# Turn order, buffers and pools of the first layer's experts, and the clearing of the rates' weights

## Chip and metric

One core of one Trainium2 chip runs the whole program. The metric is the device time of one execution in microseconds (us); it is the median of the runs, given with the lowest and the highest.

## What is computed

A hybrid diffusion trunk of two layers (`DEPTH` = 2) over 512 latent tokens (`SEQ`) and 256 context tokens (`CTX_LEN`) of width 1024, all in float32. Each layer has two sub-layers, each behind an RMSNorm that the condition modulates:

1. three token mixers on one input projection (differential attention with axial rotary, RWKV-7 in both directions, a gated convolution of width 3), gated, merged and projected;
2. a mixture of 16 SwiGLU experts of width 1024. Every expert picks its own tokens: of n tokens the 2n/16 with the highest router softmax, so 64 latent tokens, and in the first layer 32 context tokens besides (the last layer has no use for its context).

```
aff = softmax(h @ router_w); gate, idx = top_k(aff^T, cap)
hid = silu(h[idx] @ w1) * (h[idx] @ w3)
out[idx] += (hid @ w2) * gate
```

The RWKV decays and rates of each direction come from low-rank products, `tanh(wl) @ w_up` and `al @ a_up`, both of rank 64.

## The kernel before

Activations stay in SBUF by blocks of 128 tokens, two of context and four of latents. A scheduler that simulates the time line sets the order of the instructions on each engine; `high_priority` raises a piece. Pools of buffers are opened and closed as a stack; a buffer that takes over another's memory waits for that one's last use.

A layer runs `rwkv_phase`, `attention`, `merge` (branches, output projection, routing of the latents) and `experts`.

**Rates.** `lora` makes the tile `ups` (`[128, 2, 2, 128]`): in part 0 the upper 64 partitions hold `w_up`, in part 1 the lower 64 hold `a_up`; the other halves must be zero, since one product over 128 partitions with `wal` (decay ranks above, rate ranks below) gives the decay from part 0 and the rate from part 1. It is cleared once in a layer, on GpSimd (L485). `load` (L509, L510), inside `pair`, brings the parts for each pair of heads by SP's queue, and `rates` multiplies them into a bank `bk`.

**Routing, first layer.** `merge` opens `xq` (seven buffers `xn` of normalised rows), `rt` (router scratch) and, in PSUM, `rtps` (`psrt`). `route` transposes a block (`pht`), multiplies it with the router's weights (`lg`) and writes `xn` to DRAM (`xnd`). `router` makes the softmax, transposes it (`pat`), takes the top 64 or 32 per expert, and turns the positions back (`ppt`, then `post` on VectorE). The latents' part runs in `merge`, the context's at the start of `experts`.

**Experts.** Groups of four experts: `pick` builds one-hot matrices `gl` and `gc` (L1607, L1615), `group_gates` turns them into gates and token numbers (`pga`, `at`) and transposes (`pgt`, `pgc`), then gathers three tiles of 128 rows from `xnd` by an indirect DMA of GpSimd (`xg`, six buffers). `gather` transposes them (`pxi`) into `xin`, with K on the partitions and, per expert, 64 latent and 32 context columns.

Per expert, `hidden` runs the two input matrices and `output` the third. Each matrix is read in four quarters of 256 rows, 1 MB each, by `load_e` through SP's queue into one of six buffers `we`; w1 and w3 go together. The stationary operand is the expert's tokens, the moving one 512 columns of weights. A latent matmul has 64 stationary columns: w1's result goes to PSUM partitions 0 to 63 of `ph`, w3's to 64 to 127. A context matmul has 32 columns and four places in `pc`. `output` does the same with `py` and `pyc`, after `phd` has transposed the hidden rows. `by_turns` sets the order of the two on each quarter: latents, context on the even ones, context, latents on the odd ones. Results of two experts are scattered back by products with `gl` transposed (`psc`), added to `xr` on VectorE.

The second layer's experts have no context (`full` is false): `by_turns` then has latents alone.

Of the kernel before, what the change touches and what calls it, by code (L numbers as in the profile page):

```python
# [8 lines left out]
F32 = mybir.dt.float32  # L9
# [10 lines left out]
P = 128  # L20
D = 1024
# [46 lines left out]
class Trunk:  # L68
# [410 lines left out]
    def lora(self, full):  # L479
        nc, rp = self.nc, self.rp  # L480
        self.wal = rp.tile([P, N], F32, name="wal", tag="wal", bufs=1)
        self.sgl = rp.tile([P, N], F32, name="sgl", tag="sgl", bufs=1)

        self.ups = rp.tile([P, 2, 2, P], F32, name="ups")
        nc.gpsimd.memset(self.ups, 0.0)  # L485

        def decay(a, n, ps):
            nc.scalar.activation(self.wal[0:64, a:a + n], ps[0:64], AF.Tanh)
            nc.vector.tensor_copy(self.wal[64:128, a:a + n], ps[64:128])

        def gate(a, n, ps):
            g = self.sgl[:, a:a + n]
            nc.scalar.activation(g, ps, AF.Tanh, scale=0.5)
            nc.vector.tensor_scalar(g, g, 0.5, 0.5, ALU.mult, ALU.add)

        return self.unit(C_WL, True, decay), self.unit(C_GL, full, gate)
# [828 lines left out]
    def merge(self, gp, full):  # L1325

        nc, tc, l = self.nc, self.tc, self.l
# [3 lines left out]
        with ExitStack() as st:  # L1331
# [11 lines left out]
            order = [b for b in (2, 3, 4, 5, 0, 1) if b * P >= a0]  # L1343
            with tc.tile_pool(reuse_waits="tile", name="br", bufs=2, side="right") as bp:
                for b, src in branches:
# [30 lines left out]
                    if b == 1:  # L1376
# [3 lines left out]
                            self.xs[x] = self.xp.tile([P, D], F32, name=f"xr{x}", tag=f"x{x}")  # L1380
                            nc.sync.dma_start(self.xs[x], self.x_src(l, x))
                        self.routing(full)
            self.xq = self.xst.enter_context(tc.tile_pool(reuse_waits="tile", name="xq", bufs=1, side="right"))
            self.xn = {b: self.xq.tile([P, D], F32, name=f"xn{b}", tag="xn", bufs=len(order) + 1) for b in order}
            self.rt = self.rst.enter_context(tc.tile_pool(reuse_waits="tile", name="rt", bufs=1, side="right"))
            wo = st.enter_context(tc.tile_pool(reuse_waits="tile", name="wo", bufs=1, side="right"))

# [10 lines left out]
            for half, blocks in ((0, lat), (1, lat), (1, ctx), (0, ctx))[:4 if full else 2]:  # L1398
                if blocks is not ctx or half == 0:
                    ws = {}  # L1400
# [117 lines left out]
    def experts(self, full):  # L1518
        nc, tc, i, l = self.nc, self.tc, self.i, self.l
# [4 lines left out]
        with ExitStack() as st:  # L1524
            if full:
                with tc.high_priority(self.route_hp):
                    for b in range(2):
                        self.route(b, self.rt)
                    self.router(1, self.rt)
            if full:  # L1530
                self.xwp = [st.enter_context(tc.tile_pool(reuse_waits="tile", name="exw", bufs=6))] * 6
                self.ew, self.n_we = {}, 0
            else:
                self.xwp += [st.enter_context(tc.tile_pool(reuse_waits="tile", name="exw2", bufs=self.exw2))] * self.exw2
# [13 lines left out]
            ahead = None  # L1548
# [74 lines left out]
    def group_gates(self, g, grp, full, aff):  # L1623

        nc, ep, psg = self.nc, self.ep, self.psg
        v = nc.vector
        gl, gc = g.gl, g.gc
        pt = psg.tile([P, 3, NE + 1], F32, name="pga", tag="g")
        self.mm_group(
            [(pt[:, pr], gl[:, b, 2 * pr:2 * pr + 2].bitcast(F32), aff[0][:, b])  # L1630
             for pr in range(2) for b in range(4)]
            + [(pt[:, 2], gc[:, b].bitcast(F32), aff[1][:, b]) for b in range(2 if full else 0)]
        )
        if full:
            at = ep.tile([P, 3], I32, name="at", tag="at", bufs=2)
            v.tensor_copy(at, pt[:, :, NE])
            g.rows = []
            for j in range(3):
                r = ep.tile([P, D], F32, name="xg", tag="xg", bufs=6)
                nc.gpsimd.indirect_dma_start(  # L1640
                    out=r[:], out_offset=None, in_=self.xnd[:, :],
                    in_offset=bass.IndirectOffsetOnAxis(ap=at[:, j:j + 1], axis=0),
                )
                g.rows.append(r)
        g.gcol = ep.tile([P, 3], F32, name="gcol", tag="gcol", bufs=2)
        for e in range(4):
            ge = 4 * grp + e
            hs = slice(64 * (e % 2), 64 * (e % 2) + 64)
            v.tensor_copy(g.gcol[hs, e // 2:e // 2 + 1], pt[hs, e // 2, ge:ge + 1])
            if full:  # L1650
                qs = slice(32 * e, 32 * e + 32)
                v.tensor_copy(g.gcol[qs, 2:3], pt[qs, 2, ge:ge + 1])
        for pr in range(2):
            pt = psg.tile([P, 4, P], F32, name="pgt", tag="g")
            for b in range(4):
                self.tr(pt[:, b], gl[:, b, 2 * pr:2 * pr + 2].bitcast(F32))
            nc.scalar.activation(g.gt[:, pr], pt.rearrange("p b t -> p (b t)"), AF.Copy)
        if full:
            pt = psg.tile([P, 2, P], F32, name="pgc", tag="g")
            for b in range(2):  # L1660
                self.tr(pt[:, b], gc[:, b].bitcast(F32))
            nc.scalar.activation(g.gct, pt.rearrange("p b t -> p (b t)"), AF.Copy)
# [42 lines left out]
    @staticmethod  # L1705
    def by_turns(latents, context, full, load, ahead=None):


        for c in range(4):
            ws = load(c)  # L1710
            if ahead and c:
                next(ahead, None)
            fs = (latents, context) if full else (latents,)
            for f in fs[::-1] if c % 2 else fs:
                f(c, *ws)

    def hidden(self, ge, full, g, ahead=None):

# [279 lines left out]
```

## Time and profile before

| | us |
|---|---|
| median of 3 runs (lowest, highest) | 3590.33 (3589.82, 3593.44) |
| the profiled execution's own time | 3593.62 |
| its span in the profile | 3591.8 |
| TensorE (PE) busy | 3332.6 (93%) |
| VectorE (DVE) busy | 1799.7 (50%) |
| ScalarE (ACT) busy | 1293.5 (36%) |
| GpSimd (POOL) busy | 1193.1 (33%) |

The profile is of one execution. A record is one instruction on an engine; its start is measured, the end of a matmul is modelled, and matmuls overlap, so the distance from one run's start to the next one's is the better measure. PEld is TensorE's weight load. PEclk is the granted clock, 1.00 at 2.4 GHz and 0.50 at 1.2 GHz. Idle time stands in brackets with what ended it. "issue" means that nothing in the profile was waited for.

### The profile page before, as it was taken

How to read it: one execution, taken by the hardware profiler on the slowest of the kernel's cores; microseconds unless marked ns; L12 is line 12 of the kernel's file. 1: busy time of each engine (PE TensorE's matmuls, PEld its weight loads, DVE VectorE, ACT ScalarE, POOL GpSimd, SP SyncE). 2: the span in 40 equal slices, each digit the busy share in tenths (PEclk: the TensorE clock that was granted, in tenths of full speed). 3: DMA queues.
4: the chain of work that ended last, by engine and by line, in shares of the span. 5: the costliest groups of instructions: out<-in, count | busy, mean ns of one | idle time of the engine just before them, and what ended most of it. 6: DMA issues, size and time to landing. Idle time of an engine off the chain costs nothing. (4 is left out here: it accounts for less than half of the span.)

```text
span 3591.8 us, 55796 instructions
## 1 busy us (share of the span) xinstructions
PE 3332.6 (93%) x20863; PEld 2243.1 (62%) x20863; DVE 1799.7 (50%) x4213; ACT 1293.5 (36%) x3234; POOL 1193.1 (33%) x1861
## 2 busy tenths in 40 slices
PE   6999999999998988999999899999899989799998
PEld 3777877777987882233333377777778968443342
DVE  5676867654665461122212556777754666412122
ACT  3455555543454221111111335556553542211111
POOL 3656565643320410000000166667654303000000
PEclk9999999999999988999999899999999989899999
DMA  5223131434106435778888620111113154599999
GB/s 179 88 70 118 36 118 58 130 116 146 48 33 215 132 124 223 292 287 327 332 312 335 216 65 28 38 38 40 45 49 102 33 180 156 211 409 409 409 409 355
DMA packets 298642, 620.92 MB, mean 173 GB/s; under 512 B 19322, under 2 KB 160596, under 8 KB 298372
## 3 DMA queue, kind: packets, MB, share of 16 engines
q1 hardware_dynamic: 294052, 604.25, 46.6%
q0 software_dynamic: 1728, 6.29, 0.5%
q10 hardware_dynamic: 2592, 6.82, 0.5%
q8 instruction: 165, 2.70, 0.3%
q14 instruction: 105, 0.86, 0.1%
HBM read 584.00 MB, written 33.29 MB: 172 GB/s over the span
## 5 line engine op out<-in xcount | busy, mean ns | idle before, releaser
L81 PE MATMUL ph<-we,xin 128*64 128x512 f32 x2048 | 514.3, 607 | 9.2 <-DVE hid L1748 5.3
L81 PE MATMUL pw<-hhi,w_hi 128*128 128x512 f32 (+1 forms) x1272 | 490.9, 390 | 20.5 <-ACT w_hi L132 8.7
L81 PE MATMUL pw<-hlo,w_hi 128*128 128x512 f32 (+1 forms) x1272 | 451.4, 359 | 0.0
L81 PE MATMUL pw<-hhi,w_lo 128*128 128x512 f32 (+1 forms) x1272 | 451.0, 360 | 0.2 <-POOL w_lo L134 0.2
L134 POOL TENSOR_TENSOR w_lo<-w_raw,w_hi 128x1024 fp32r<-128x1024 f32 x124 | 298.0, 2409 | 350.2 <-ACT w_hi L132 278.3
L81 PEld LDWEIGHTS ph<-we,xin 128*64 128x64 f32 x2048 | 150.3, 139 | 330.0 <-issue 316.0
L1853 POOL TENSOR_TENSOR ylo<-y,yhi 128x512 fp32r<-128x512 f32 x28 | 35.2, 1279 | 884.4 <-ACT yhi L1852 884.4
L735 DVE TENSOR_TENSOR wt<-slot,lvm 128x256 f16<-128x256 f32 x576 | 231.3, 419 | 133.9 <-PE slot L81 110.9
L81 PEld LDWEIGHTS pw<-hhi,w_hi 128*128 128x128 f32 x1272 | 243.4, 193 | 48.9 <-ACT w_hi L132 9.8
L81 PEld LDWEIGHTS pw<-hlo,w_hi 128*128 128x128 f32 x1272 | 243.3, 193 | 33.1 <-issue 13.9
L81 PEld LDWEIGHTS pw<-hhi,w_lo 128*128 128x128 f32 x1272 | 241.2, 191 | 33.6 <-issue 1.0
L132 ACT ACTIVATE w_hi<-w_raw 128x1024 fp32r<-128x1024 f32 x168 | 176.9, 1056 | 235.6 <-DMA w_raw<-in_w_in 68.7
L81 PE MATMUL py<-we,hT 128*64 128x512 f32 x1024 | 247.6, 604 | 7.7 <-DMA we<-in_exp_w 2.4
L752 ACT ACTIVATE xx<-slot 128x256 f16<-128x256 f32 x384 | 146.4, 382 | 162.0 <-PE slot L81 139.8
L1747 ACT ACTIVATE sl<-ph 64x512 f32<-64x512 f32 x64 | 37.7, 590 | 439.7 <-PE ph L81 421.6
L1863 DVE TENSOR_TENSOR xr<-xr,psc 128x512 f32<-128x512 f32 x144 | 90.7, 683 | 201.5 <-PE psc L81 201.4
L81 PEld LDWEIGHTS py<-we,hT 128*64 128x64 f32 x1024 | 70.3, 138 | 151.5 <-issue 134.1
L81 PE MATMUL pt<-w_hi,hhi 128*128 128x256 f32 x544 | 155.9, 288 | 4.9 <-ACT xk L1123 2.0
L81 PE MATMUL slot<-xt,wt 128*128 128x128 f16 x960 | 133.1, 224 | 28.7 <-DVE wt L735 27.5
L81 PE MATMUL pt<-w_lo,hhi 128*128 128x256 f32 x544 | 155.7, 287 | 3.5 <-POOL w_lo L134 3.5
L81 PE MATMUL pt<-w_hi,hlo 128*128 128x256 f32 x544 | 155.0, 285 | 0.0
L1748 DVE TENSOR_TENSOR hid<-sl,ph 64x512 f32<-64x512 f32 x64 | 44.2, 690 | 208.7 <-ACT sl L1747 208.2
(420 smaller groups left out, 7558.2 us busy)
## 6 DMA issues: line engine op xcount, KB each, us to landing
we<-in_exp_w SPq DMA_DIRECT2D x384, 1024.0 KB
w_raw<-in_w_in SPq DMA_DIRECT2D x124, 512.0 KB
ada_w<-in_ada_w SPq DMA_DIRECT2D x96, 512.0 KB
w_raw<-in_w_branch SPq DMA_DIRECT2D x24, 512.0 KB
w_raw<-in_w_out SPq DMA_DIRECT2D x20, 512.0 KB
gd<-gt SPq DMA_DIRECT2D x24, 384.0 KB
g<-gd SPq DMA_DIRECT2D x24, 384.0 KB
gd<-gt SPq DMA_DIRECT2D x24, 256.0 KB
```

Source lines behind the costliest of these rows:

```text
L81: return self.leg(self.nc.tensor.matmul(out, lhsT, rhs, start=start, stop=stop))
L132: nc.scalar.activation(hi, raw, AF.Copy)
L134: self.lo_eng.tensor_tensor(lo, raw, hi.bitcast(F32), ALU.subtract)
L735: v.tensor_tensor(wt, ps, self.lvm[:, :, l], ALU.mult)
L752: nc.scalar.activation(x, ps2, AF.Copy)
L1747: nc.scalar.activation(sl, ph[0:64, ns], AF.Silu)
L1748: v.tensor_tensor(hid[0:64, ns], sl, ph[64:128, ns], ALU.mult)
L1853: (v if by_block else self.ylo_eng[nh]).tensor_tensor(lo, yn, hi.bitcast(F32), ALU.subtract)
L1863: v.tensor_tensor(x, x, pt, ALU.add)
```

## The change

`by_turns` runs the latents on quarters 0 and 1, the context on 0 to 3, then the latents on 2 and 3; a quarter is loaded at its first use. The weights have eleven buffers. To make room, `xq` and the router's pools are closed before the weight pool is opened, `xn` has one buffer less in the first layer, and `xg` three buffers. In `lora` only the halves of `ups` that no load writes are cleared.

```diff
--- before.py
+++ after.py
@@ -482,7 +482,8 @@
         self.sgl = rp.tile([P, N], F32, name="sgl", tag="sgl", bufs=1)
 
         self.ups = rp.tile([P, 2, 2, P], F32, name="ups")
-        nc.gpsimd.memset(self.ups, 0.0)
+        nc.gpsimd.memset(self.ups[64:128, 0], 0.0)
+        nc.gpsimd.memset(self.ups[0:64, 1], 0.0)
 
         def decay(a, n, ps):
             nc.scalar.activation(self.wal[0:64, a:a + n], ps[0:64], AF.Tanh)
@@ -1380,8 +1381,9 @@
                             self.xs[x] = self.xp.tile([P, D], F32, name=f"xr{x}", tag=f"x{x}")
                             nc.sync.dma_start(self.xs[x], self.x_src(l, x))
                         self.routing(full)
-            self.xq = self.xst.enter_context(tc.tile_pool(reuse_waits="tile", name="xq", bufs=1, side="right"))
-            self.xn = {b: self.xq.tile([P, D], F32, name=f"xn{b}", tag="xn", bufs=len(order) + 1) for b in order}
+            self.xq = (self.rst if full else self.xst).enter_context(
+                tc.tile_pool(reuse_waits="tile", name="xq", bufs=1, side="right"))
+            self.xn = {b: self.xq.tile([P, D], F32, name=f"xn{b}", tag="xn", bufs=len(order) + 1 - full) for b in order}
             self.rt = self.rst.enter_context(tc.tile_pool(reuse_waits="tile", name="rt", bufs=1, side="right"))
             wo = st.enter_context(tc.tile_pool(reuse_waits="tile", name="wo", bufs=1, side="right"))
 
@@ -1527,8 +1529,8 @@
                     for b in range(2):
                         self.route(b, self.rt)
                     self.router(1, self.rt)
-            if full:
-                self.xwp = [st.enter_context(tc.tile_pool(reuse_waits="tile", name="exw", bufs=6))] * 6
+                self.rst.close()
+                self.xwp = [st.enter_context(tc.tile_pool(reuse_waits="tile", name="exw", bufs=11))] * 11
                 self.ew, self.n_we = {}, 0
             else:
                 self.xwp += [st.enter_context(tc.tile_pool(reuse_waits="tile", name="exw2", bufs=self.exw2))] * self.exw2
@@ -1636,7 +1638,7 @@
             v.tensor_copy(at, pt[:, :, NE])
             g.rows = []
             for j in range(3):
-                r = ep.tile([P, D], F32, name="xg", tag="xg", bufs=6)
+                r = ep.tile([P, D], F32, name="xg", tag="xg", bufs=3)
                 nc.gpsimd.indirect_dma_start(
                     out=r[:], out_offset=None, in_=self.xnd[:, :],
                     in_offset=bass.IndirectOffsetOnAxis(ap=at[:, j:j + 1], axis=0),
@@ -1706,13 +1708,16 @@
     def by_turns(latents, context, full, load, ahead=None):
 
 
-        for c in range(4):
-            ws = load(c)
-            if ahead and c:
-                next(ahead, None)
-            fs = (latents, context) if full else (latents,)
-            for f in fs[::-1] if c % 2 else fs:
-                f(c, *ws)
+        ws = {}
+        order = [(latents, c) for c in range(4)]
+        if full:
+            order[2:2] = [(context, c) for c in range(4)]
+        for f, c in order:
+            if c not in ws:
+                ws[c] = load(c)
+                if ahead and c:
+                    next(ahead, None)
+            f(c, *ws[c])
 
     def hidden(self, ge, full, g, ahead=None):
```

The rows of an order count matmuls; of the float32 ones here the profile has two records each. TensorE in the first layer's experts, the second half of one expert's hidden part and the output part after it, before (`ph`, `py`: latents; `pc`, `pyc`: context; `xin`, `hT`: the tokens):

```order
L81 MATMUL ph<-we,xin 64x512 x8
L81 MATMUL pc<-we,xin 32x512 x2
L81 MATMUL ph<-we,xin 64x512 x7
L81 MATMUL pc<-we,xin 32x512 x8
L81 MATMUL ph<-we,xin 64x512
L81 MATMUL pc<-we,xin 32x512 x6
L81 MATMUL ph<-we,xin 64x512 x7
L81 MATMUL py<-we,hT 64x512 x4
L81 MATMUL pyc<-we,hT 32x512 x8
L81 MATMUL py<-we,hT 64x512 x8
L81 MATMUL pyc<-we,hT 32x512 x8
L81 MATMUL py<-we,hT 64x512 x4
```

and one expert's hidden part and the output part after it, now:

```order
L81 MATMUL ph<-we,xin 64x512 x16
L81 MATMUL pc<-we,xin 32x512 x32
L81 MATMUL ph<-we,xin 64x512 x16
L1774 MATMUL phd<-ident,hid 128x96 x8
L81 MATMUL py<-we,hT 64x512 x8
L81 MATMUL pyc<-we,hT 32x512 x16
L81 MATMUL py<-we,hT 64x512 x8
```

The latents' first half and second half now stand together, with the whole context between them.

TensorE at the start of the first layer's experts, before (`lg`, `pht`: the context's router; `pga`, `pgt`: group 0's picking):

```order
L108 MATMUL pht<-ident,xr_13928 128x128 x4
L85 MATMUL pga<-aff_14582,gl 128x17
L108 MATMUL pgt<-ident,gl 128x128 x2
L85 MATMUL pga<-aff_14582,gl 128x17
L108 MATMUL pgt<-ident,gl 128x128 x2
L85 MATMUL pga<-aff_14582,gl 128x17
L85 MATMUL lg<-rws,h_15565 128x16 x2
L85 MATMUL pga<-aff_14582,gl 128x17
L85 MATMUL lg<-rws,h_15565 128x16
L85 MATMUL pga<-aff_14582,gl 128x17
L85 MATMUL lg<-rws,h_15565 128x16
L85 MATMUL pga<-aff_14582,gl 128x17 x3
```

and now:

```order
L108 MATMUL pht<-ident,xr_13929 128x128 x4
L85 MATMUL lg<-rws,h_15566 128x16 x4
L108 MATMUL pht<-ident,xr_13929 128x128 x4
L85 MATMUL lg<-rws,h_15596 128x16 x4
L85 MATMUL lg<-rws,h_15607 128x16 x4
L1500 MATMUL pat<-ident,aff_14584 16x128 x2
L1516 MATMUL ppt<-ident,pos 128x16 x2
L85 MATMUL pga<-aff_14583,gl 128x17
L108 MATMUL pgt<-ident,gl 128x128 x2
L85 MATMUL pga<-aff_14583,gl 128x17
L108 MATMUL pgt<-ident,gl 128x128 x2
L85 MATMUL pga<-aff_14583,gl 128x17
```

The picking moved behind the router's last transposes (`pat`, `ppt`).

SP's queue at the same place, before (`arow`, `rows`: gates and parameters of the next layer):

```order
L128 DMA w_raw<-in_w_out 128x4x256 x7
L1700 DMA we<-in_exp_w 128x2x1024 x6
L381 DMA arow<-ard_2_89 128x512
L305 DMA rows<-in_norm_g 8x128 x2
L305 DMA rows<-in_rwkv_conv_w 36x128
```

and now:

```order
L128 DMA w_raw<-in_w_out 128x4x256 x7
L1702 DMA we<-in_exp_w 128x2x1024 x11
L381 DMA arow<-ard_2_89 128x512
L305 DMA rows<-in_norm_g 8x128 x2
L305 DMA rows<-in_rwkv_conv_w 36x128
```

Five more weight loads stand ahead of the small ones. Elsewhere the order differs in the first load of `ups` in the first layer, which moved ahead of the eight loads of `arow`, and in the last heads of the second layer's attention; TensorE's order up to the first layer's experts and from the second layer's merge on is the same.

## Rows read from the trace of the kernel before

**Rows 1.** Head of the page.

```profile
span 3591.8 us, 55796 instructions
```

**Rows 2.** Stretches: us, engines' busy us (records), PEclk, DMA share, GB/s.

```profile
1420.00:2020.00 600.00, 595.02 (x3233) 191.36 (x3234) 143.86 (x248) 86.86 (x168) 33.98 (x29) 0.99 0.84 315
3150.00:3550.00 400.00, 382.51 (x1762) 153.42 (x1760) 81.90 (x143) 52.89 (x97) 17.64 (x14) 0.98 1.03 409
2890.00:2940.00 50.00, 38.38 (x223) 31.33 (x222) 39.98 (x96) 31.65 (x76) 2.81 (x6) 0.85 0.58 209
```

**Rows 3.** Timeline of TensorE, first experts: start us, us, engine, line, instruction, records.

```profile
1628.00 7.09 PE L81 MATMUL ph<-we,xin 128*64 128x512 f32 x32
1635.02 3.64 PE L81 MATMUL pc<-we,xin 128*32 128x512 f32 x32
1638.59 3.65 PE L81 MATMUL ph<-we,xin 128*64 128x512 f32 x16
1642.17 0.88 PE L1769 MATMUL phd<-ident,hid 96*128 96x96 f32 x8
```

**Rows 4.** Timeline of TensorE, another expert.

```profile
1445.11 1.05 PE L81 MATMUL pc<-we,xin 128*32 128x512 f32 x4
1446.09 3.65 PE L81 MATMUL ph<-we,xin 128*64 128x512 f32 x14
1449.67 1.92 PE L81 MATMUL pc<-we,xin 128*32 128x512 f32 x16
1451.52 1.07 PE L81 MATMUL ph<-we,xin 128*64 128x512 f32 x2
1452.52 1.91 PE L81 MATMUL pc<-we,xin 128*32 128x512 f32 x12
1454.36 3.65 PE L81 MATMUL ph<-we,xin 128*64 128x512 f32 x16
```

**Rows 5.** Groups by form, 1300 to 2150 us: busy us, mean ns, idle before.

```profile
L81 PE MATMUL ph<-we,xin 128*64 128x512 f32 x1024 | 258.5, 605 | 3.0 <-DVE hid L1748 2.8 <-ACT xin L1684 0.2
L81 PE MATMUL pc<-we,xin 128*32 128x512 f32 x1024 | 141.5, 600 | 0.0
L81 PE MATMUL py<-we,hT 128*64 128x512 f32 x512 | 128.4, 612 | 3.2 <-issue 1.8 <-DVE hT L1770 1.0 <-ACT sl L1747 0.4
...
L81 PE MATMUL pyc<-we,hT 128*32 128x512 f32 x512 | 64.5, 598 | 0.7 <-ACT hT L1770 0.7
```

**Rows 6.** Timeline of TensorE, start of the first experts.

```profile
1330.12 0.45 PE L85 MATMUL pga<-aff,gl 128*128 128x17 f32 x2
...
1334.46 1.44 PE L85 MATMUL pga<-aff,gl 128*128 128x17 f32 x6
...
1337.48 3.43 PE L85 MATMUL lg<-rws,h 128*128 128x16 f32 x16
```

**Rows 7.** Timeline of VectorE (DVE), the same start.

```profile
1336.87 1.43 DVE L1607 TENSOR_TENSOR gl<-iota,post 128x256 fp32r<-128x256 f32 x4 [1.98 <-PE pgt L108]
...
1349.15 0.19 DVE L1515 COPY post<-ppt 128x32 f32<-128x32 f32 x1 [0.55 <-PE ppt L1514]
...
1350.90 0.16 DVE L1636 CAST at<-pga 128x3 int32<-128x3 f32 x1 [1.03 <-PE pga L85]
```

**Rows 8.** Stretches at the same start, columns as in rows 2.

```profile
1330.00:1335.00 5.00, 5.00 (x27) 5.00 (x25) 1.22 (x3) 0.00 (x0) 0.00 (x0) 0.50 1.02 400
1345.00:1350.00 5.00, 0.64 (x4) 0.57 (x5) 4.04 (x13) 0.00 (x0) 0.00 (x0) 0.50 0.00 0
```

**Rows 9.** Timeline of TensorE, first `bk` of each layer; in brackets the idle time.

```profile
71.94 1.19 PE L81 MATMUL bk<-wal,ups 128*128 128x256 f32 x2 [4.67 <-DMA ups<-in_rwkv_w_up]
...
2075.61 0.67 PE L81 MATMUL bk<-wal,ups 128*128 128x256 f32 x2 [1.90 <-DMA ups<-in_rwkv_w_up]
```

**Rows 10.** Timeline of GpSimd (POOL), the clear of `ups` in each layer.

```profile
69.27 0.52 POOL L485 MEMSET ups<- 128x512 f32 x1
...
2072.99 0.52 POOL L485 MEMSET ups<- 128x512 f32 x1
```

## The prediction

> **What bounds the kernel now.** I went from the whole to one wave of matmuls. The profiled execution spans 3591.8 us [rows 1] and took 3593.62 us; the median of the runs shown, 3590.33 us, lies 3.3 us below. I read the stretches next. In the first layer's experts, from 1420 to 2020 us, TensorE is busy 595.02 of 600 us while the weights stream at 315 GB/s; in the second layer's experts, from 3150 to 3550 us, the same kind of transfer runs at 409 GB/s [rows 2]. So the changed stage is bound by TensorE and has spare transfer rate. A fully busy engine may still be badly filled, so the third view is the timeline of TensorE inside that stage. A latent matmul uses 64 columns of the array and a context matmul 32, so two latent or four context matmuls can run side by side; I call such a set a wave. Each matmul leaves two records.
>
> A run of 32 `ph` records takes 7.02 us from its start to the next run's, one of 16 takes 3.58 us [rows 3]. The 16 more records, four waves, cost 3.44 us: **0.86 us a wave**. What is left, 3.58 less four waves, is **0.14 us for each change of kind**. A context run of 32 records, four waves of four matmuls, takes 3.57 us: the same two prices. The next group shows what the order of before wastes: seven latent matmuls (14 records) take 3.58 us like eight, six context matmuls (12 records) take 1.84 us against 1.85 for eight (16 records), two of them (4 records) take 0.98 us, and a single latent one (2 records) 1.00 us [rows 4]. A wave that isn't full costs a whole wave.
>
> **The change, part by part.**
>
> *By turns.* Before, latents and context alternated on each quarter of a matrix and the scheduler cut the runs further; now the order on TensorE is mostly 16, 32, 16 matmuls in the hidden half and 8, 16, 8 in the output half. TensorE runs its instructions in that order, so I count runs and waves in both programs, from the first `ph` to the first transpose of the second layer. Both have 768 latent and 768 context matmuls; `ph` and `pc` have 1024 records each, `py` and `pyc` 512 [rows 5], two to a matmul. Before: 119 latent runs with 410 waves, 97 context runs with 216 waves. After: 58 runs with 389 waves, 46 runs with 199 waves. That is 626 - 588 = 38 waves and 216 - 104 = 112 runs less: 38 x 0.86 = 32.7 us and 112 x 0.14 = 15.7 us, together **-48.4 us**. As a check, before comes to 626 x 0.86 + 216 x 0.14 = 568.6 us, where the four groups are busy 258.5 + 141.5 + 128.4 + 64.5 = 592.9 us, tails and stretches at half clock included [rows 5].
>
> The Trainium skill ("TensorEngine Tiling (Array Packing)", Key Properties) says that a change of tiling mode drains the engine, and names no other cost of a mixed order there. By it the gain would be the 15.7 us of the runs alone; the half-filled waves above are what the trace adds to it.
>
> The other work on TensorE there (`psc`, `phd`, `pxi`) keeps its count and is only grouped otherwise; after it TensorE waits for evictions. Of such waits all kinds together leave 600 - 595.02 = 5.0 us idle [rows 2], so I take 0, between -5 and +5.
>
> *Eleven buffers.* Five more weight loads stand on SP's queue at the start, ahead of the rows and gate loads behind them. One load is 1.05 MB; at the 400 GB/s that such loads reach there [rows 8] it takes 2.6 us, five take 13.1 us. The transfers stand still from 1345 to 1350 us [rows 8], before the gather of token rows, so most of it fits. Bounds 0 and +13; I take 0, nearest to the empty row. With four quarters at most held at once by an expert, seven loads can be ahead instead of four. The stage must now move its 315 GB/s x 600 us = 189 MB in about 556 us (the stage's part of the gain taken off): 340 GB/s, under the 409 seen. So no new wait for weights.
>
> *Pools closed earlier.* Group 0's picking (`gl`, `pga`, `pgt`) now stands behind the context's router, not in the midst of it, since their buffers are the router's. Before, TensorE went from the first `pga` at 1330.12 us to the router's last 16 `lg` records at 1337.48 us [rows 6]; of these 7.36 us eight `lg` records at 3.43/16 = 0.21 us and four transposes at about the same (2.6 us) are the router's, so it now ends 4.8 us earlier. Behind the chain's end (`post`, 1349.15 us) the token numbers `at` followed 1.75 us later [rows 7]; now there is first one of four `gl` (1.43/4), then 24 records at the price of the six `pga` in 1.44 us (5.8 us at most), and the next group's four `gl` on VectorE (1.43 us [rows 7]): about 7.2 us. Net 7.2 - 1.75 - 4.8 = +0.7; I take **+1 us**, bounds -3 (VectorE's part hidden) and +3. Three gather buffers instead of six cost nothing: the old rows are transposed long before the next group's are gathered.
>
> *Clearing.* The first `bk` matmul of each layer waited for its loads, which waited for a whole clear on GpSimd: TensorE stood 4.67 us until 71.94 us, and 1.90 us until 2075.61 us [rows 9]. Now only the rows no load writes are cleared, so the loads go ahead, but the matmul still waits for the clears, which GpSimd does at the same place in its order: they started at 69.27 and 2072.99 us and took 0.52 us [rows 10]. Two halves end by 70.3 and 2074.0 us at the latest, 1.6 us sooner each. I take **-3 us**; bounds 0 (it comes back in the wait for the next product) and -6.6 (both waits gone).
>
> *The last heads of the second layer* are reordered by the scheduler near 2890 to 2940 us, where TensorE is busy 38.38 of 50 us [rows 2]. Same work, so 0; half of the idle 11.6 us either way, +-6.
>
> Sum: -48.4 + 0 + 0 + 1 - 3 + 0 = -50.4 us. Against the profiled execution that is 3543.2 us; against the median **3540 us**. That is 1.4%; a measurement of this kernel tells a change from none beyond about 0.2%, 7 us.
>
> **The rivals.**
>
> *Only the drains are saved.* If half-filled waves overlapped with what follows once the order differs, 15.7 us would remain, with -3 and +1: 3572.6 us. Against it: in rows 4 every partial run, before either kind, costs its full wave. 0.06.
>
> *Weights late.* A load waits on SP for a freed buffer, and the queue behind it waits too; with half the latents held back until the context's end, buffers come free in clumps. If arrivals ran at 330 GB/s, the 189 MB would take 573 us, 27 us less than 600 instead of 44: 3557 us. For it: 1.05 MB loads issued in clumps; against: the 409 GB/s of the second layer under the same loads. 0.11.
>
> The Trainium skill ("DMA: Bandwidth & Descriptors", Bandwidth) measures 341 GB/s for single 1 MB transfers and puts the limit of the memory per core at some 358 GB/s when its neighbour is busy too. By the first figure the stage would just be fed, with nothing over; the 409 GB/s row on this one core disagrees.
>
> *Slower.* If the weights and not the array set the pace of this stage already, 315 GB/s is its ceiling, fuller waves only turn into waiting, and the five loads at the start push the gather back by their full 13.1 us: 3590.3 + 13.1 - 3 + 1 = 3601 us. It decides as soon as the stage can't pass 315 GB/s. Against it: 409 GB/s, and almost no idle time of TensorE. 0.03.
>
> That the change doesn't do what it says is excluded for the order, which stands in the program; I leave 0.01 for what I haven't seen.
>
> **How the numbers follow.** The forecast has 0.79. Its own bounds (regrouping +-5, start -3 to +16, clearing -3.6 to +3, heads +-6) won't all fall together: some 12 us below and 14 above, 3528 to 3554. To hold 8 in 10 with part of the late weights I give 3527 to 3560. Faster by over 0.2%: the forecast, the drains alone and the late weights, 0.79 + 0.06 + 0.11 = 0.96; slower: 0.03; within 0.2%: the 0.01 left.
>
> **What would show it.** In the first layer's experts: `ph` runs of 32 records and `pc` runs of 64 without a cut, each at 0.86 us a wave; the stage about 48 us shorter, TensorE still over 98% busy, transfers near 340 GB/s, no wait of `ph` or `py` for `we`. At the start, `at` within 3 us of 1351, the weights' transfers done before the gather. The `bk` waits at 70 and before 2030 us near 3 us and near zero. I am wrong if matmuls wait for weights, if runs stay 16 and 32 but cost more than 0.86 us a wave, or if the gather lands over 5 us later.

## The result and the profile after

| | us |
|---|---|
| the changed kernel, median of 4 runs (lowest, highest) | 3529.64 (3527.93, 3537.01) |
| the kernel before, beside it, median of 4 | 3591.69 (3589.82, 3593.44) |
| ratio, 95% interval | 0.9835 (0.9823 to 0.9847) |
| profiled execution of the changed kernel | 3529.81, span 3528.0 |

The forecast was 3540 us with a range of 3527 to 3560. Run once more later (e11), on one chip with e10 and e12, the changed kernel took 3536.53 us (3532.22 to 3538.74, 4 runs) against 3589.46 (15 runs), a ratio of 0.9854 (0.9839 to 0.9869). Its single runs reach from 3528 to 3539 us; the forecast's ratio, 3540 / 3590.33 = 0.9860, lies inside the second interval and just above the first. Why executions of one program lie so far apart is a part of what follows.

The head of the page of the changed kernel, and its line of busy times; TensorE lost 63.0 us of busy time, while VectorE, ScalarE and GpSimd changed by 1.3 us at most:

```profile
span 3528.0 us, 55804 instructions
...
PE 3269.6 (93%) x20863; PEld 2235.1 (63%) x20863; DVE 1799.8 (51%) x4213; ACT 1293.9 (37%) x3234; POOL 1194.4 (34%) x1863
```

Stretches of the changed kernel, first layer's experts and second layer's (columns as in rows 2):

```profile
1400.00:1960.00 560.00, 554.67 (x3266) 195.10 (x3262) 143.01 (x248) 87.63 (x168) 33.88 (x29) 0.99 0.86 333
...
3086.00:3486.00 400.00, 382.27 (x1760) 153.21 (x1758) 81.70 (x142) 52.88 (x97) 17.66 (x14) 0.98 1.03 409
```

TensorE is busy 554.67 of 560 us, the weights stream at 333 GB/s, and the second layer still moves 409 GB/s, as in [rows 2]. The timeline of TensorE in one expert:

```profile
1510.65 7.07 PE L81 MATMUL pc<-we,xin 128*32 128x512 f32 x64
1517.65 7.09 PE L81 MATMUL ph<-we,xin 128*64 128x512 f32 x32
1524.67 0.88 PE L1774 MATMUL phd<-ident,hid 96*128 96x96 f32 x8
```

The eight context waves take 7.00 us from start to start and the eight latent ones after them 7.02 us; [rows 3] had 7.02 us for eight latent waves. The prices of a wave and a change of kind are those of before. The groups by form over the first layer's experts (1300 to 2080 us):

```profile
L81 PE MATMUL ph<-we,xin 128*64 128x512 f32 x1024 | 233.1, 598 | 3.0 <-DVE hid L1753 2.8 <-ACT xin L1686 0.2
L81 PE MATMUL py<-we,hT 128*64 128x512 f32 x512 | 122.0, 605 | 3.6 <-issue 2.6 <-DVE hT L1775 1.0
L81 PE MATMUL pc<-we,xin 128*32 128x512 f32 x1024 | 115.2, 595 | 0.0
L81 PE MATMUL pyc<-we,hT 128*32 128x512 f32 x512 | 65.1, 597 | 0.6 <-ACT hT L1775 0.6
```

Against [rows 5], `ph` fell from 258.5 to 233.1 us, `pc` from 141.5 to 115.2, `py` from 128.4 to 122.0, `pyc` stayed. Nothing waits for `we`. The records are as many as before; the time went because fewer waves run part empty and the kind changes less often.

To see where the 63.8 us of span went I cut both executions at the same instructions. In brackets: how much of the stretch the trace records at half clock, 0.50.

| from, to | before | after | after, second profile (e11) |
|---|---|---|---|
| start, first `bk` | 71.94 | 70.72 | 70.17 |
| first `bk`, last `po` (first layer's mixers) | 1247.56 (64.2) | 1240.02 (51.2) | 1241.35 (54.1) |
| last `po`, first `ph` (start of the experts) | 41.02 (36.6) | 43.23 (39.6) | 43.06 (39.0) |
| first `ph`, last `py` (the stage) | 666.79 (18.0) | 615.57 (11.6) | 619.13 (19.0) |
| last `py`, first `bk` of the second layer | 48.30 (27.3) | 46.01 (20.5) | 45.40 (17.1) |
| that `bk`, first `ph` of the second layer | 1025.04 (78.5) | 1020.78 (75.1) | 1021.23 (68.3) |
| that `ph`, end | 491.18 (18.5) | 491.67 (18.8) | 492.25 (29.1) |

The stage gives 51.2 of the 63.8 us. The mixers of the first layer give 7.5 us, though TensorE runs the same instructions there in the same order; the prediction had nothing for that stretch behind its first wait. The second layer up to its experts gives 4.3 us. In the stage TensorE is almost always busy, so a us at half clock loses half a us of work. Less half of its half-clock time the stage is 666.79 - 9.0 = 657.8 us before, 615.57 - 5.8 = 609.8 us after, and 619.13 - 9.5 = 609.6 us in the second profile. This **net stage time** is what the experiments below are read by. It fell by 48.0 us. Profiles of one order on TensorE agree in it to 0.2 us: 657.8, 657.7 and 657.7 us in before, e3 and e9, and 609.8, 609.8 and 609.6 us in the changed kernel, e4 and e11.

At the start, TensorE of the changed kernel, and VectorE from `post` to `at`:

```profile
1326.31 1.89 PE L85 MATMUL lg<-rws,h 128*128 128x16 f32 x8 [0.78 <-ACT h L1467]
...
1336.04 0.36 PE L1516 MATMUL ppt<-ident,pos 16*128 16x16 f32 x2 [5.47 <-DVE pos L1513]
1337.02 0.61 PE L85 MATMUL pga<-aff,gl 128*128 128x17 f32 x2 [0.62 <-DVE gl L1609]
...
1339.42 2.15 PE L85 MATMUL pga<-aff,gl 128*128 128x17 f32 x10
...
1349.41 0.87 PE L108 MATMUL pxi<-ident,xg 128*128 128x128 f32 x3 [6.15 <-DMA xg<-xnd,at]
```

```profile
1336.44 0.19 DVE L1517 COPY post<-ppt 128x32 f32<-128x32 f32 x1 [0.55 <-PE ppt L1516]
1336.55 1.42 DVE L1609 TENSOR_TENSOR gl<-iota,post 128x256 fp32r<-128x256 f32 x4
...
1343.47 0.15 DVE L1638 CAST at<-pga 128x3 int32<-128x3 f32 x1
```

`post` to `at` takes 7.03 us, with `gl`, twenty records of `pga` and transposes inside it, where [rows 7] had 1.75. From the last `po` to `post` it is 25.7 us for 29.6, since the picking is out of the router's way; the sum of both is 32.7 us for 31.4. At 1342 to 1344 us, before the gather, the transfers are down to 38 GB/s: the weights are in by then. At the first `bk` of each layer (TensorE, first layer; then VectorE and GpSimd beside it; then TensorE and GpSimd, second layer):

```profile
70.72 0.70 PE L81 MATMUL bk<-wal,ups 128*128 128x256 f32 x2 [2.46 <-POOL ups L485]
```

```profile
69.30 1.17 DVE L490 COPY wal<-pw 64x256 f32<-64x256 f32 x2 [5.25 <-ACT wal L489]
```

```profile
70.36 0.31 POOL L485 MEMSET ups<- 64x256 f32 x1
70.72 0.30 POOL L486 MEMSET ups<- 64x256 f32 x1
```

```profile
2015.55 0.67 PE L81 MATMUL bk<-wal,ups 128*128 128x256 f32 x2 [1.57 <-issue]
```

```profile
2013.37 0.31 POOL L485 MEMSET ups<- 64x256 f32 x1
2013.74 0.30 POOL L486 MEMSET ups<- 64x256 f32 x1
```

The wait fell from 4.67 to 2.46 us and from 1.90 to 1.57 us [rows 9]. In the first layer `bk` starts at 70.72 us, when the first clear is done (70.36 + 0.31 = 70.67 us); it doesn't wait for the second, which ends at 71.02. In the second layer both clears are done by 2014.04 us, 1.5 us before `bk`. There `bk` starts 0.1 us after the first of VectorE's two copies of `wal` is done (2015.44 us) and before the second is. The first copy of the first layer is done at 69.73 us, so clears that were done earlier could win up to some 0.9 us at the first place and nothing at the second.

### The profile page after: what moved, and what is told of

Read it like the earlier page. It is cut to its first block, busy times and chain, and to the rows that moved or that the text cites. A ratio compares the mean times of both kernels' runs of the same rounds, so it can differ in the third digit from the quotient of the medians.

```text
span 3528.0 us, 55804 instructions
## 1 busy us (share of the span) xinstructions
PE 3269.6 (93%) x20863; PEld 2235.1 (63%) x20863; DVE 1799.8 (51%) x4213; ACT 1293.9 (37%) x3234; POOL 1194.4 (34%) x1863
## 5 line engine op out<-in xcount | busy, mean ns | idle before, releaser
L81 PE MATMUL ph<-we,xin 128*64 128x512 f32 x2048 | 489.2, 603 | 9.4 <-DVE hid L1753 5.3
L757 ACT ACTIVATE xt<-slot 128x256 f16<-128x256 f32 x384 | 146.7, 383 | 0.0
```

What stands on the lines that cost most here:

```text
L81: return self.leg(self.nc.tensor.matmul(out, lhsT, rhs, start=start, stop=stop))
L757: nc.scalar.activation(xt, ps, AF.Copy)
```

## The experiments

Every kernel was counted like the two of the prediction: waves and runs of one kind in TensorE's order, in the first layer's experts. The model gives 0.86 us to a wave and 0.14 us to a run; the other work of the stage is 609.8 - (588 x 0.86 + 104 x 0.14) = 89.6 us, taken once from the changed kernel and then left alone. The net stage is that of one profile for each kernel.

| kernel | waves, runs | model, us | stage (half clock) | net stage | us by the median | ratio to before |
|---|---|---|---|---|---|---|
| before | 626, 216 | 658.2 | 666.79 (18.0) | 657.8 | 3591.69 | 1 |
| changed | 588, 104 | 609.8 | 615.57 (11.6) | 609.8 | 3529.64 | 0.9835 |
| e1: old turns, else changed | 588, 166 | 618.5 | 626.48 (15.2) | 618.9 | 3545.94 | 0.9876 |
| e2: before, new turns | 669, 268 | 702.5 | 704.00 (14.7) | 696.6 | 3624.24 | 1.0103 |
| e3: before, new clearing | 626, 216 | 658.2 | 667.07 (18.8) | 657.7 | 3584.85 | 0.9990 |
| e4: whole clear, else changed | 588, 104 | 609.8 | 619.44 (19.3) | 609.8 | 3538.54 | 0.9852 |
| e5: latent waves half empty | 584, 106 | 606.7 | 613.15 (12.9) | 606.7 | 3530.76 | 0.9839 |
| e6: more runs | 587, 162 | 617.1 | 622.83 (11.6) | 617.0 | 3546.65 | 0.9880 |
| e7: eight buffers, else changed | 611, 138 | 634.4 | 641.04 (14.2) | 633.9 | 3557.44 | 0.9908 |
| e9: before, new pools | 626, 216 | 658.2 | 666.72 (18.0) | 657.7 | 3589.49 | 1.0004 |
| e10: changed, waves tied | 576, 97 | 598.5 | 600.99 (5.9) | 598.0 | 3524.53 | 0.9824 |
| e11: changed, again | 588, 104 | 609.8 | 619.13 (19.0) | 609.6 | 3536.53 | 0.9854 |
| e12: before, waves tied | 630, 273 | 669.6 | 675.15 (11.6) | 669.3 | 3595.51 | 1.0017 |

The model is within 0.6 us of the net stage time in every kernel but e2. Each ratio is to the runs of before beside it; the intervals reach 0.0008 to 0.0019 to either side. The times expected for the kernels that are built on the changed one count from its first median, 3529.64 us. By theory A all six (e1, e4 to e7, e10) came out 3 to 10 us above them, in line with the second median, which is 6.9 us higher; so the net stage is the sharper reading.

**e1 and e2: turns or buffers?** Each undoes one of the two against one of the kernels. e1 is the changed kernel with the old loop:

```diff
-        ws = {}
-        order = [(latents, c) for c in range(4)]
...
+        for c in range(4):
+            ws = load(c)
...
+            for f in fs[::-1] if c % 2 else fs:
+                f(c, *ws)
```

> The changed kernel with the old order in by_turns (latents and context alternate on each quarter); eleven buffers, pools and clearing stay. Counted in TensorE's order of the first layer's experts, this program has 588 waves, as the changed kernel has, and 166 runs of one kind where that has 104. Theory A (a wave costs 0.86 us full or not, a change of kind 0.14 us): 62 runs more, 62 x 0.14 = 8.7 us above the changed kernel, so 3538 us; most of the gain would then come with the buffers, since with them the scheduler no longer cuts waves. Rival B (the order of the turns is what gains, the buffers only feed it): 48 us above the changed kernel, 3578 us. Rival C (each change of kind costs more than 0.14 us because the array drains): 0.3 us each would give 3548 us.

e2 is the kernel before with the new loop and nothing else (the same lines the other way).

> The kernel before with the new order in by_turns alone; six buffers, pools and clearing as before. Counted in TensorE's order, the first layer's experts have 669 waves and 268 runs, where the kernel before has 626 and 216. Theory A: 43 x 0.86 + 52 x 0.14 = 37.0 + 7.3 = 44 us slower than before, 3635 us, and more if weights come late besides. Rival B (the order itself gains): near 3543 us. The stretch from 72 to 1320 us has the same instructions as in the kernel before: if its half-clock stretches near 454, 576 and 593 us return at the same places, they belong to the program; if not, they come and go from execution to execution.

e1 kept most of the gain: its net stage is 9.1 us above the changed kernel's (8.7 expected), the median 0.9876 (0.9859 to 0.9894) of before. Rival B's 48 us are excluded. Its median lies 8 us over the 3538 us expected, and 9 us over the changed kernel's second median. By the median alone rival C (3548 us) would lie nearer; the net stage, 9.1 us up and not the 18.6 us of rival C, is against it, and e6 comes back to it. e2 is slower than before by 1.03% (1.0087 to 1.0119), its net stage by 38.9 us. So the order of the turns by itself costs 39 us with six buffers and gains 9 us with eleven; the buffers (with the pools and the clearing, which leave the net stage as it is, e9 and e3) gain 38.9 us with the old order and 86.8 with the new. The timeline of TensorE in e2 shows how (`pc` x4 is half a wave of context, `ph` x2 half a wave of latents):

```profile
1723.82 1.05 PE L81 MATMUL pc<-we,xin 128*32 128x512 f32 x4
1724.80 1.07 PE L81 MATMUL ph<-we,xin 128*64 128x512 f32 x2
1725.81 0.30 PE L1772 MATMUL phd<-ident,hid 96*128 96x96 f32 x1
1726.04 1.91 PE L81 MATMUL pc<-we,xin 128*32 128x512 f32 x12
```

0.98 us and 1.01 us from start to start, as in [rows 4]: half-filled waves again, only more of them. The chip didn't wait for weights; over 640 us of e2's stage TensorE is busy 638.08 us:

```profile
1400.00:2040.00 640.00, 638.08 (x3232) 196.94 (x3228) 141.86 (x244) 85.62 (x165) 33.88 (x29) 0.99 0.78 295
```

What the buffers change is the order that the scheduler writes. That it writes these cuts because, with six, weights are late by its own reckoning is my reading, and not tried; that the cuts are in the order and that no matmul waits for weights on the chip is what the runs show. e2 alone misses the model, by 5.9 us; TensorE is idle 5.23 us in its stage where before has 7.77, so 2.5 us of that is other work covering waits. The other 3.4 us stay open.

**e3 and e4: the clearing.** e3 adds the two smaller clears to the kernel before, e4 takes them out of the changed kernel:

```diff
-        nc.gpsimd.memset(self.ups, 0.0)
+        nc.gpsimd.memset(self.ups[64:128, 0], 0.0)
+        nc.gpsimd.memset(self.ups[0:64, 1], 0.0)
```

> The kernel before with the new clearing of ups alone. TensorE's order is that of before. Theory A: the first bk wait goes from 4.67 to about 2.5 us, the half-clock stretch behind it gets about 1 us cheaper, the second layer's wait loses 0.3 us: 3.5 us faster, 3588 us. Rival D (the whole 8.5 us by which the changed kernel is ahead at the end of the first layer's mixers comes from the clearing, by half-clock stretches that no longer occur): 9 us faster, 3583 us, with those stretches missing between 400 and 800 us.

> The changed kernel with the whole clear of ups as before. Theory A: the first bk wait is 4.7 us again, 3.5 us above the changed kernel, 3533 us. Rival D: 9 us above it, 3538.5 us, with half-clock stretches near 454, 576 and 593 us as in the kernel before.

e3 took 0.999 (0.998 to 1.0001) of before: 3.3 us by the medians, not told apart from none. Nor do e4's 3538.54 us (3531.86 to 3542.13) decide, since the changed kernel's own two medians are 7 us apart. Both medians lie nearer to rival D's numbers (3583 and 3538.5) than to theory A's, so the profiles have to decide. The first `bk` starts at 71.8 to 72.6 us in the five profiles with the whole clear and at 69.8 to 70.8 us in the eight with the small ones, 1.7 us apart by the means. The way from there to the last `po` shows no effect: 1240.5 to 1247.6 us with the whole clear, 1237.8 to 1249.1 us with the small ones, over the same instructions. Rival D falls: e2, with before's program, took 1242.32 us there for before's 1247.56, and e7, with the small clears, 1249.12 us.

What goes with the time is the half-clock share: 41.0 us of e3's 1237.83, 68.3 us of e7's 1249.12. Less half of it, the thirteen ways are 1213.1 to 1218.2 us, so it takes up about half of their spread. The half-clock stretches also answer e2's expectation: of those near 454, 576 and 593 us in before, e2 has the first two and e9 the first; with the small clears the first two stand in e1, e6, e7, e10 and e11 and are missing in e3, e5 and the changed kernel's first profile. They come and go, and the small clears don't remove them. Two stretches of four profiles show it, 570 to 600 us and the whole way from 72 to 1320 us (PEclk is the third number from the end). The kernel before:

```profile
570.00:600.00 30.00, 26.46 (x175) 21.63 (x174) 20.28 (x62) 14.01 (x41) 16.74 (x30) 0.89 0.28 89
72.00:1320.00 1248.00, 1187.30 (x8476) 1012.62 (x8476) 774.67 (x1856) 567.15 (x1501) 566.65 (x901) 0.97 0.31 98
```

e2, the same program up to the experts:

```profile
570.00:600.00 30.00, 26.71 (x192) 21.54 (x191) 20.36 (x64) 15.53 (x46) 17.52 (x34) 0.94 0.28 88
72.00:1320.00 1248.00, 1182.54 (x8478) 1008.16 (x8478) 779.88 (x1876) 568.90 (x1503) 569.55 (x902) 0.98 0.31 99
```

The changed kernel, first and second profile:

```profile
570.00:600.00 30.00, 27.35 (x206) 22.10 (x206) 22.24 (x65) 16.87 (x49) 17.56 (x34) 1.00 0.28 88
72.00:1320.00 1248.00, 1184.05 (x8490) 1009.64 (x8489) 783.21 (x1888) 568.18 (x1503) 569.86 (x903) 0.98 0.31 101
```

```profile
570.00:600.00 30.00, 27.86 (x198) 22.75 (x198) 20.60 (x61) 17.57 (x50) 15.21 (x30) 0.94 0.25 80
72.00:1320.00 1248.00, 1184.68 (x8488) 1010.30 (x8486) 781.49 (x1887) 568.09 (x1503) 569.06 (x903) 0.98 0.31 100
```

The clock of 570 to 600 us is 0.89 and 0.94 for one program, 1.00 and 0.94 for the other. The Trainium skill ("TensorE: Matmul & The Clock Gate", What's actually happening) says that the gate's watch runs freely and doesn't start with the kernel, so that the point of a change varies. These four profiles agree with it as far as they go: the clock differs between executions of one program. That this is the reason is not shown by any run here.

**e5 and e6: what a wave and a run cost.** e5 leaves w3's latent products out for most of the inner dimension, so that a wave has one latent matmul in place of two; e6 deals the context out in two pieces.

```diff
-                    self.mm(ph[64:128, ns], xl[:, k], w3[:, kk, ns], k == 0, k == 7)
+                    if not full or k in (0, 7):
+                        self.mm(ph[64:128, ns], xl[:, k], w3[:, kk, ns], k == 0, k == 7)
```

> The changed kernel, in whose first layer the w3 products of the latents are left out for the inner products 1 to 6 of 8 (192 of the 1536 latent and context matmuls of the first layer's experts; all weights are still loaded). Two consecutive w1 products then want the same columns. Theory A (a wave costs 0.86 us full or not): 584 waves and 106 runs where the changed kernel has 588 and 104, so 3 us faster, 3526 us, with a quarter of the latent work gone. Rival (each matmul has its own price, half a wave, 0.43 us): 192 x 0.43 = 82 us faster, 3447 us. Measured by the stage, first ph to last py, less half of its time at half clock: 609.8 us in the changed kernel, so 607 against 528 us.

```diff
-            order[2:2] = [(context, c) for c in range(4)]
+            C = [(context, c) for c in range(4)]
+            order = order[:2] + C[:2] + order[2:3] + C[2:] + order[3:]
```

> The changed kernel with the turns latents 0 and 1, context 0 and 1, latents 2, context 2 and 3, latents 3: waves 587 where the changed kernel has 588, runs 162 where it has 104. Theory A: 58 x 0.14 - 0.86 = 7.3 us slower, 3537 us; the stage, less half of its time at half clock, 617 us where the changed kernel has 609.8. Rival C (a change of kind costs 0.3 us): 16.5 us slower, 3546 us, stage 626 us. Rival (changes of kind are free, waves are all): 3529 us, stage 609 us.

e5's timeline of TensorE, and its `ph` group:

```profile
1511.76 7.07 PE L81 MATMUL pc<-we,xin 128*32 128x512 f32 x64
1518.77 7.08 PE L81 MATMUL ph<-we,xin 128*64 128x512 f32 x20
1525.78 0.88 PE L1775 MATMUL phd<-ident,hid 96*128 96x96 f32 x8
```

```profile
L81 PE MATMUL ph<-we,xin 128*64 128x512 f32 x640 | 230.3, 604 | 3.0 <-DVE hid L1754 2.8 <-ACT xin L1686 0.2
```

A run of 20 records takes 7.01 us where one of 32 took 7.02: eight waves both. The group has 640 records for 1024 and is busy 230.3 us for 233.1. The net stage is 606.7 us, as the wave model says, 79 us above what a price for each matmul gives. In e6 58 more runs and one wave less cost 7.2 us of net stage, (7.2 + 0.9) / 58 = 0.14 us a run: free changes and changes at 0.3 us both fall. Its median, 3546.65 us (3538.56 to 3551.89), is 10 us over the 3537 us expected; in its profile the first layer's mixers, which the edit doesn't touch, took 1247.52 us for the changed kernel's 1240.02.

**e7 and e9: buffers, pools and the start.** e7 has eight weight buffers in the changed kernel (`bufs=8))] * 8`), e9 the new pools in the kernel before (`xq` in `rst`, `rst` closed before `exw` opens, `xn` and `xg` smaller).

> The changed kernel with eight weight buffers for eleven. The program then has 611 waves and 138 runs where the changed kernel has 588 and 104. Theory A with the buffers acting through the scheduler's order: 23 x 0.86 + 34 x 0.14 = 24.5 us slower, 3554 us, stage less half of its half-clock time 634 us, without waits for weights. Rival (the buffers act by transfers that come late on the chip): TensorE idle before matmuls on weights, and the stage longer than 634 us. Start of the first layer's experts, last output projection to first ph: 43.2 us as in the changed kernel if the order of the picking costs the 2.2 us, some 41.7 us if the loads in front of the gather do (two more than before for five).

> The kernel before with the pools of the change alone: the router's pools and xn closed before the weights' pool opens, one xn buffer less, three xg buffers; six weight buffers, old turns, whole clear. The order in the stage is that of before (626 waves, 216 runs). Theory A: the start, last output projection to first ph, takes 43.2 us where before takes 41.0, the stage stays at 657.8 us less half of its half-clock time: 2.2 us slower, 3590 us. Rival (the five loads ahead of the gather cost the 2.2 us, not the pools): start 41.0 us, time that of before.

e7's net stage is 633.9 us, 24.1 above the changed kernel. Its groups show no wait for weights:

```profile
L81 PE MATMUL ph<-we,xin 128*64 128x512 f32 x1024 | 243.6, 600 | 3.0 <-DVE hid L1753 2.7 <-ACT xin L1686 0.2
L81 PE MATMUL pc<-we,xin 128*32 128x512 f32 x1024 | 131.0, 595 | 0.0
```

So the buffers act through the order alone. The start surprised me: 41.58 us in e7 and 41.49 in e9, not 43.2, and in both the picking stands in the midst of the context's router as before. TensorE and VectorE of e9:

```profile
1328.10 1.44 PE L85 MATMUL pga<-aff,gl 128*128 128x17 f32 x6
...
1331.12 3.43 PE L85 MATMUL lg<-rws,h 128*128 128x16 f32 x16
...
1350.16 0.90 PE L108 MATMUL pxi<-ident,xg 128*128 128x128 f32 x3 [5.36 <-DMA xg<-xnd,at]
```

```profile
1342.79 0.19 DVE L1515 COPY post<-ppt 128x32 f32<-128x32 f32 x1 [0.55 <-PE ppt L1514]
...
1344.55 0.16 DVE L1637 CAST at<-pga 128x3 int32<-128x3 f32 x1 [1.04 <-PE pga L85]
```

`pga` runs ahead of the router's last `lg`, and `post` to `at` takes 1.76 us. So not the closed pools but the buffers beyond eight put the picking behind the router. That its tiles then find room only in the router's memory is read from the pools and wasn't tried. Of the 2.2 us, 0.5 come with the pools (e9), the other 1.7 with the late picking. The pools as the whole cause fall. The totals lie near what the loads ahead of the gather were to give (41.0 and some 41.7 us), but the way behind the loads doesn't bear them out: from `at` to the first `pxi`, over the gather, it is 5.94 us with eleven loads (5.68 to 6.08 over seven profiles), 5.70 with eight (e7) and 5.62 with six (e9): some 0.3 us. The longer part lies before `at`, in the picking: 32.7 us from the last `po`, for 31.4 in before, e7 and e9.

**e10 to e12: waves tied.** The model has 576 waves as the least, 384 + 192. In the changed kernel's order about half of the cut waves break off at a transpose of the picking or the gathering. e10 ties a wave together:

```diff
+    def wave(self, full, mms):
+        first = self.mm(*mms[0])
+        for m in mms[1:]:
+            if full:
+                with self.tc.high_priority(self.wave_hp), self.tc.issue_after(first.ins):
+                    self.mm(*m)
...
-                    self.mm(ph[0:64, ns], xl[:, k], w1[:, kk, ns], k == 0, k == 7)
-                    self.mm(ph[64:128, ns], xl[:, k], w3[:, kk, ns], k == 0, k == 7)
+                    self.wave(full, [(ph[0:64, ns], xl[:, k], w1[:, kk, ns], k == 0, k == 7),
+                                     (ph[64:128, ns], xl[:, k], w3[:, kk, ns], k == 0, k == 7)])
```

and the same for `pc`, `py` and `pyc`, with `wave_hp` 2000. e11 is the changed kernel again, e12 the tie in the kernel before.

> The changed kernel, in which the matmuls of one wave in the first layer's experts (two latent, four context) are tied together: those behind the first are raised in priority and issued after it, so that no other work cuts a wave. Counted in TensorE's order, 576 waves and 97 runs where the changed kernel has 588 and 104; 576 is the least, 384 + 192. Theory A: 12 x 0.86 + 7 x 0.14 = 11.3 us faster than the changed kernel, 3518 us; the stage, first ph to last py, less half of its time at half clock, 598.5 us where the changed kernel has 609.8. Rival (the transfers or the evictions bind now): the stage stays above 604 us and TensorE waits for weights.

> The changed kernel once more, for a second profile and more rounds on the same chip as the version with whole waves. If the half-clock stretches between 72 and 1320 us come and go from execution to execution, this profile has others there than the first one, and the way from the first bk to the last output projection differs from 1240 us by several us; less half of the half-clock time it is again 1213 to 1218 us. The stage is 609.8 us less half of its half-clock time, the start 43.2 us.

> The kernel before with the tied waves alone: six buffers, old turns. Counted in TensorE's order, 630 waves and 273 runs where the kernel before has 626 and 216. Theory A: 4 x 0.86 + 57 x 0.14 = 11.4 us slower than before, 3600 us, the stage 669 us less half of its half-clock time: without buffers the scheduler can't keep waves whole, since it places a matmul only when its weights are there by its reckoning. Rival (the tie alone makes waves full): 43 us faster than before.

e10 beats both kernels: 3524.53 us (3523.09 to 3527.31, 5 runs), 0.9824 (0.9811 to 0.9838) of before, where e11, on the same chip beside it, took 3536.53 us. Its slowest run is 5 us below e11's fastest; against the changed kernel's first comparison (0.9835) the intervals overlap. The net stage fell by 11.8 us (11.3 expected). TensorE's timeline in one expert, and the stretch of the stage:

```profile
1500.93 7.09 PE L81 MATMUL ph<-we,xin 128*64 128x512 f32 x32
1507.95 7.07 PE L81 MATMUL pc<-we,xin 128*32 128x512 f32 x64
1514.95 7.09 PE L81 MATMUL ph<-we,xin 128*64 128x512 f32 x32
1521.97 0.88 PE L1783 MATMUL phd<-ident,hid 96*128 96x96 f32 x8
...
1526.80 3.64 PE L81 MATMUL pyc<-we,hT 128*32 128x512 f32 x32
```

```profile
1380.00:1950.00 570.00, 561.88 (x3366) 197.77 (x3366) 146.33 (x257) 88.55 (x171) 33.91 (x29) 1.00 0.87 337
```

In this expert the runs are 32, 64, 32 and 16, 32, 16 records without a cut, TensorE is busy 561.88 of 570 us, and 337 GB/s still don't bind. e11's way through the first layer's mixers, 1241.35 us, is only 1.3 us from the first profile's and not several, as expected; less half of its half-clock time it is 1214.3 us, inside the 1213 to 1218 us expected. e12 is slower than before, 1.0017 (1.0007 to 1.0026): with six buffers the tie alone leaves 630 waves and cuts more runs. The buffers come first.

## Why the prediction came out as it did

**The prices were right.** 0.86 us a wave and 0.14 us a change of kind, read off [rows 3, 4], give -48.4 us for the stage; the net stage fell by 48.0, and the two prices, with the other work taken from the changed kernel, then met the net stage of eleven further profiles to 0.6 us each (seven other orders and the changed one again), e2 excepted. "Only the drains are saved" (-15.7) falls by the stage itself and by e5; a change of kind costs 0.14 us in e6 and is the smaller part. The Trainium skill ("TensorEngine Tiling (Array Packing)", Key Properties) names a drain at a change of tiling mode; the trace agrees that such a change costs time. "Weights late" and "slower" fall by 333 GB/s without a wait for `we`.

**The step that failed is the heading above the sum.** "By turns" was given the whole -48.4 and "Eleven buffers" 0, because the counts were taken from the two finished programs and not from either edit alone. The runs share them out the other way: eleven buffers bring the waves from 626 to 588 and the runs from 216 to 166 (e1, -38.9 us of net stage), the turns the runs from 166 to 104 (-9.1). Taken first, the turns cost 38.9 us (e2), and the buffers then give 86.8; the gain is of both together. The sum didn't suffer, since a count of the finished program holds whichever edit made it.

**The start** cost 2.2 us for +1, inside its bounds of -3 and +3. The reckoning of `post` to `at` was good (7.03 us for 7.2), but the router ended 3.9 us earlier, not 4.8, and from `at` to the first `pxi` it took 5.94 us, for 5.19 before. That it came from the pools was wrong (e9). `at` came at 1343.47 us, not "within 3 us of 1351", since the last `po` already came 8.8 us earlier; between the two 1.3 us were lost.

**The clearing** was taken at -3, two times 1.6. The first layer gave 1.7 us by the means over thirteen profiles; in the second the wait fell by 0.33 us, not 1.6. The failed step is "1.6 us sooner each": it left out that `bk` also needs the first copy of `wal`, which ended the wait in the second layer (2015.44 us), 1.4 us after the clears were done. So "near zero" didn't come there: 1.57 us.

**The last heads** were taken at 0 within 6. The three profiles with before's order of the second layer took 1025.0 to 1027.3 us there (before, e3, e9), the four with the changed kernel's 1020.8 to 1023.9 (both of it, e4, e7), 3.4 us less by the means; the six with other orders 1021.1 to 1025.3. Inside the bounds, with as much clock in it as order; it wasn't tried by itself.

**The 10 us between forecast and first median** are mostly clock. Between the two profiled executions 63.8 us were gained for 50.4 forecast: 7.5 us in the mixers, 4.3 in the second layer up to its experts and 2.8 in the stage lie above the forecast, 1.2 at the start below it. By half of the half-clock time, 6.5 us of the mixers, 1.7 of the second layer's stretch and 3.2 of the stage's 51.2 go with half-clock stretches that the first profiled execution of the changed kernel happened not to have. That is luck and not the edit: the second profile has 19.0 us at half clock in the stage, before has 18.0. The second median, 53 us below before, is within 3 us of the forecast's gain.

## What to carry to other kernels

Where small matmuls share TensorE's columns, count waves and changes of kind, not matmuls: read both prices from two runs of different length in the timeline, then count them in the finished order, where an edit's effect on time can be had before a run. If a scheduler writes that order, ask what it believes to be late; more buffers can pay through the order it writes, with no wait on the chip to show for it. Cutting one execution at the same instructions as another, with the half-clock time of each stretch beside it, keeps luck with the clock out of the account.

## What the runs showed of the hardware

- The first layer's mixers, one order on TensorE in all thirteen profiles, took 1237.8 to 1249.1 us, with 41.0 to 68.3 us of them at half clock. A single profile can't tell an edit of 5 us there.
- In the second layer's experts half clock left no mark on the time: 11.4 us of it in 492.26 us in e4, 29.1 us in 492.29 us in e10. There the DMA engines are busy throughout (share 1.03, 409 GB/s), and in the changed kernel's 400 us above `ph` and `py` wait 5.2 us for `we`.
- A latent matmul of `py` and one of `ph` can make one wave. In the changed kernel a `py` record starts at 1502.78 us and a `ph` record beside it at 1502.79 us, where the one run ends and the next begins.
